# Retention output channel-major in 256-token blocks, PSUM banks given out by the scheduler, and the LRU in three steps

## The chip, the cores and the metric

The kernel runs on the 8 cores of one Trainium2 chip, each core taking one of the 8 sequences of the batch. The metric is the device time of the slowest core, in microseconds (us). Cores 0 to 3 are one die, cores 4 to 7 the other.

Engines are named as in the profile: PE multiplies matrices (PEld loads its weights), DVE is the vector engine, ACT the scalar engine with its function tables (a load of one took 1283 ns in the stage studied below), POOL the GpSimd engine, SP a queue for transfers. PE's results land in PSUM, which the kernel uses as 8 banks of 128 x 512 f32; the program lets PE write a bank again only after another engine has read it out (an *eviction*).

Some executions of this program, whatever the kernel, fall into a slower state, in which a die has a lower granted clock.

## The reference

A layer of a hybrid decoder, per sequence 2048 tokens of 1024 channels. Only the middle part is touched by the change:

```python
x = x + 0.5 * swiglu(rmsnorm(x, ffn1_norm), ffn1_w1, ffn1_w3, ffn1_w2)      # first FFN
h = rmsnorm(x, mix_norm)
u = h @ w_in                                        # q | k | v | g_ret | x_lru | g_lru

# mixer A: retention, 4 heads, dk 128, dv 256
ret = retention_chunkwise(rotary(q, pos), rotary(k, pos), v)   # chunks of 128 tokens and a running state
ret = head_groupnorm(ret, ret_gn)                   # (y - mean) * rsqrt(var + eps) over the 256 of a head
y_ret = (silu(g_ret) * ret) @ w_ret_o

# mixer B: convolution of 4 taps and a gated linear recurrence (called LRU below)
xc = causal_depthwise_conv(x_lru, conv_w, conv_b)
r, i = sigmoid(xc @ w_r + b_r), sigmoid(xc @ w_i + b_i)        # blocks of 128
log_a = -8 * r * softplus(-lam);  a = exp(log_a);  mult = sqrt(1 - a * a)
hl = scan(h_t = a_t * h_(t-1) + mult_t * i_t * xc_t)
y_lru = (hl * gelu(g_lru)) @ w_lru_o

gates = sigmoid(h @ w_branch_gate + b_branch_gate)  # from here on called the tail
x = x + (gates[:D] * y_ret + gates[D:] * y_lru) @ w_out
# ... memory cross-attention, second FFN, final norm
```

## The kernel before

The kernel is written as a list of operations for each engine, with the handles that each reads and writes. A list scheduler in the Python code gives every engine a fixed order: it works with assumed durations and takes, at every step, the operation that can start first. The chip then runs these orders, with semaphores between the engines. PSUM banks are handed out before that, in fixed pools, round robin:

```python
def lru_units():                      # (cut)
    bk = Banks([0, 1])
def ret_steps():
    bkp = Banks([2, 3, 7])            # projections
    bkm = Banks([5, 6])               # scores, outputs, transposes
    SBANK = 4                         # the running state
```

A unit of the LRU is one block of 128 channels and 1024 tokens (16 units), all in one piece:

```python
def unit(u):                          # (cut: only what each engine does)
    # PE: x_lru -> ACT: copy to XL;  DVE: tensor_scalar + 3 scalar_tensor_tensor (conv taps) -> XC
    # POOL: cast to XCB;  PE: g_lru -> ACT: Gelu -> GG (two slots);  PE: gates -> ACT: Tanh -> TR, TI
    dve(lambda e: e.scalar_tensor_tensor(xc.ap, ti.ap, 1.0, xc.ap, ALU.add, ALU.mult), ...)
    act(mu.ap, tr.ap, AF.Exp, ...)
    act(tr.ap, tr.ap, AF.Exp, ...)
    act(mu.ap, mu.ap, AF.Ln, ...)
    act(mu.ap, mu.ap, AF.Exp, ...)    # mu = sqrt(1 - a*a), by Exp and Ln
    pool(lambda e: e.tensor_tensor(mu.ap, xc.ap, mu.ap, ALU.mult), ...)
    prev = XC.v(((u + 1) % 2) * 1024 + 1023, 1)      # last column of the other half of XC
    dve(lambda e: e.tensor_tensor_scan(xc.ap, tr.ap, mu.ap, prev.ap, ALU.mult, ALU.add), ...)
    pool(lambda e: e.tensor_tensor(bt.ap, xc.ap, gg.ap, ALU.mult), ...)
```

Retention is token-major: the output of a chunk is 128 tokens x 2 heads of 256 channels. It is normalised over the free axis and then transposed by PE for the next product:

```python
def fin(p, c, retb, sg, gn_):         # (cut)
    for h in range(2):
        dve(lambda e, h=h: e.bn_stats(...))          # mean and variance of 256 columns
    for h in range(2):
        dve(lambda e, h=h: e.bn_aggr(...))
    dve(lambda e: e.tensor_tensor(s[:, 16:18], mv[:, :, 1], ep, ALU.add), ...)
    pool(lambda e: e.tensor_tensor(s[:, 18:20], s[:, 16:18], ..., ALU.pow), ...)   # (var + eps) ** -0.5
    for h in range(2):
        dve(lambda e, h=h: e.tensor_scalar(rn..., banks[retb]..., mean, rstd, ALU.subtract, ALU.mult), ...)
    pool(lambda e: e.tensor_tensor(at.ap, rn.ap, sg.ap, ALU.mult), ...)

def at_out(p, d, ats):                # 8 transposes on PE, 4 copies with a scale on ACT

def vg(p, c):                         # (cut) value and gate projections of a chunk
    act(sg.ap, banks[outs[1]][:, :], AF.Tanh, [hbk[outs[1]]], sg.hs, 512, tab=S_TANH, scale=0.5)
    dve(lambda e: e.scalar_tensor_tensor(sg.ap, sg.ap, 1.0, banks[outs[1]][:, :], ALU.add, ALU.mult), ...)

for s in range(16):
    unit(s)
    step(s // 8, s % 8)
tail()
```

The softmax here doesn't subtract the row's maximum and nothing guards it: scores larger than these inputs give would overflow.

Of the kernel before, what the change touches and what calls it, by code (L numbers as in the profile page):

```python
# [26 lines left out]
class H:  # L27
    __slots__ = ("name", "lw", "lr")

    def __init__(self, name=""):  # L30
        self.name = name
        self.lw = None
        self.lr = []


class Op:
    __slots__ = ("eng", "fn", "id", "deps", "raw", "cost", "tab", "dma", "succ", "nd", "ready", "fin",
                 "st", "pos", "marked", "idx", "sem", "semval", "prev", "clock", "key")


class Prog:
    def __init__(self):
        self.ops = []

    def add(self, eng, fn, reads=(), writes=(), cost=0.0, tab=None, dma=0, key=None):
        op = Op()
        op.eng, op.fn, op.id, op.cost, op.tab, op.dma = eng, fn, len(self.ops), cost, tab, dma
        op.key = op.id if key is None else key
        deps = {}
        for h in reads:  # L50
            if h.lw is not None:
                deps[h.lw.id] = (h.lw, True)
        for h in writes:
            if h.lw is not None:
                deps[h.lw.id] = (h.lw, True)
            for r in h.lr:
                deps[r.id] = (r, True)
        for h in reads:
            h.lr.append(op)
        for h in writes:  # L60
            h.lw = op
            h.lr = []
        op.deps = [d for d, _ in deps.values()]
        op.raw = {i for i, (_, t) in deps.items() if t}
        self.ops.append(op)
        return op


    def schedule(self):
# [16 lines left out]
        pend = {e: [] for e in ENGS}  # L86
# [5 lines left out]
        cnt = [0]  # L92

        def push(op):
            cnt[0] += 1
            heapq.heappush(pend[op.eng], (op.ready, op.key, cnt[0], op))

        for op in ops:
            if op.nd == 0:
                push(op)  # L100
        left = len(ops)

        def candidate(e):
            p, a = pend[e], avail[e]
            t = tfree[e]
            while p and p[0][0] <= t:
                r, k, c, op = heapq.heappop(p)
                heapq.heappush(a, (k, c, op))
            if e == "act":
                best = None  # L110
                for (k, c, op) in a:
                    pen = TAB_NS + TAB_HOLD if (op.tab is not None and tab[0] is not None and tab[0] not in op.tab) else 0.0
                    cand = (t + pen, k, c, op)
                    if best is None or cand[:3] < best[:3]:
                        best = cand
                for (r, k, c, op) in p:
                    pen = TAB_NS + TAB_HOLD if (op.tab is not None and tab[0] is not None and tab[0] not in op.tab) else 0.0
                    cand = (r + pen, k, c, op)
                    if best is None or cand[:3] < best[:3]:
                        best = cand  # L120
                return best
            if a:
                k, c, op = a[0]
                return (t, k, c, op)
            if p:
                r = p[0][0]
                best = None
                for (rr, k, c, op) in p:
                    if rr <= r + 1e-6 and (best is None or (k, c) < (best[1], best[2])):
                        best = (rr, k, c, op)  # L130
                return best
            return None

        while left:
            sel = None
            for e in ENGS:
                c = candidate(e)
                if c is not None and (sel is None or c[0] < sel[0]):
                    sel = c
                    se = e  # L140
            assert sel is not None, "deadlock"
            st, k, c, op = sel
            a, p = avail[se], pend[se]
            done = False
            for i, x in enumerate(a):
                if x[2] is op:
                    a[i] = a[-1]
                    a.pop()
                    heapq.heapify(a)
                    done = True  # L150
                    break
            if not done:
                for i, x in enumerate(p):
                    if x[3] is op:
                        p[i] = p[-1]
                        p.pop()
                        heapq.heapify(p)
                        break
            st = max(tfree[se], op.ready)
            if se == "act" and op.tab is not None:  # L160
# [5 lines left out]
            tfree[se] = end  # L166
# [4 lines left out]
            op.fin = end  # L171
            op.st = st
            op.pos = len(order[se])
            order[se].append(op)
            left -= 1
            for s in op.succ:
                s.nd -= 1
                lat = 0.0 if (s.eng == op.eng and not op.dma and op.id not in s.raw) else SEM_NS
                if end + lat > s.ready:
                    s.ready = end + lat  # L180
                if s.nd == 0:
                    push(s)
        self.order = order
        self.span = max(op.fin for op in ops)
        return order

    def emit(self, nc):
        order = self.schedule()
# [15 lines left out]
        todo = sorted(self.ops, key=lambda o: (o.fin, o.id))  # L204
# [3 lines left out]
        while n < total:  # L208
            moved = False
            for e in ENGS:  # L210
                while ptr[e] < len(order[e]):
# [9 lines left out]
                    for d in deps:  # L221
# [3 lines left out]
                        else:  # L225
                            if d.eng == e and (e == "pe" or d.id not in op.raw) and not op.dma:
# [81 lines left out]
ARENA_KB = 198  # L308
# [42 lines left out]
T = 2048  # L351
# [14 lines left out]
KB = 1024  # L366

# [7 lines left out]

S_SILU = (18,)
# [4 lines left out]
S_LN = (6,)  # L381

# [20 lines left out]
def build(stage=None):  # L403
    if stage is None:
        stage = STAGE
    nc = bass.Bass("TRN2", target_bir_lowering=False)
    P = Prog()
# [8 lines left out]
    wl_d = dram("w_lru_in", [KC, 128, 2 * KC * 128])  # L416
    wqk_d = dram("w_qk", [2, 128, KC * 512])
    wv_d = dram("w_v", [2, 128, KC * 512])
    wg_d = dram("w_g", [2, 128, KC * 512])
    wgate_d = dram("w_gate", [128, 2 * KC * 128])  # L420
# [12 lines left out]
    v_dr = nc.dram_tensor("v_scr", [128, 4 * 2 * D], BF16).ap()  # L433
    h_park = [H("park%d" % i) for i in range(16)]
# [13 lines left out]
    maskf = fixed("maskf", 128, F32)  # L448
    gam = fixed("gam", 64, F32)
    epst = fixed("epst", 64, F32)  # L450
    cst = fixed("cst", 16, F32)
    wgate = fixed("wgate", 2 * KC * 128, BF16)
    stat_t = nc.alloc_sbuf_tensor("stat", [128, 16 * 4], F32)
    h_stat = [H("stat%d" % i) for i in range(16)]
    rst_t = nc.alloc_sbuf_tensor("rstat", [128, 4 * 24], F32)
    h_rst = [H("rst%d" % i) for i in range(4)]
    io_i = fixed("io_i", 128, I32)
    io_f = fixed("io_f", 128, F32)

    A = Arena(nc, ARENA_KB)  # L460
    banks = [nc.alloc_psum_tensor("bank%d" % i, [128, 512], F32) for i in range(8)]
    hbk = [H("bank%d" % i) for i in range(8)]

    class Banks:
        def __init__(self, ids):
            self.ids = ids
            self.i = 0

        def next(self):
            b = self.ids[self.i % len(self.ids)]  # L470
            self.i += 1
            return b
# [13 lines left out]
    RT = A.buf("RT", 182 * KB, F32, 4 * TB)  # L486
    MT = A.buf("MT", 182 * KB, BF16, KC * MEM)
# [83 lines left out]

    def consts_early():
# [862 lines left out]
```

## Time and profile before

The median was 1898.67 us (1897.75 to 1900.28, three runs). These lines of the profile's page show busy time of each engine over the whole span, and busy tenths in 40 slices of 47.4 us; PEclk is the TensorE clock that was granted, in tenths of full speed.

```profile
PE 1728.3 (91%) x8416; PEld 813.6 (43%) x8584; DVE 906.9 (48%) x1354; ACT 607.0 (32%) x964; POOL 388.3 (20%) x435
...
PE   4999999999987887679688999999999999999997
...
DVE  3476332333486677676785122255553432233355
ACT  3321111112245654565556212135441111111122
...
PEclk9999999999999888889889999999999999999998
```

The average of 91% hides two different kernels. In most slices of the FFNs and the tail PE is busy for 47.0 to 47.2 of 47.4 us at a granted clock of 1.00, so next to nothing is to be gained there. In slices 12 to 22 retention and LRU are mixed (*the stage*): PE falls to 6 to 8 tenths in all but one, its clock to 8 in seven of them, and DVE rises to 5 to 8.

I call *the stage* the time from the end of the first FFN's last matmul to the first matmul that reads the tail's weights. The windows view gives one line for it: start and end, length, then busy us of PE, PEld, DVE, ACT and POOL (with instruction counts), mean PE clock, DMA share and GB/s.

```profile
540.60:1005.80 465.20, 358.60 (x1776) 169.27 (x1808) 333.16 (x480) 261.09 (x406) 200.88 (x149) 0.89 0.11 25
```

PE is busy for 359 of 465 us, and those 359 us include work at half speed (in this core's stage the clock records stand at 0.5 for 106 us, and PE is busy for 59 of them). No other engine is full: the next, DVE, is busy for 333 us. The list of PE's waits in the stage says on whom it waits (us in total, times, longest us):

```profile
PE bank L514 <- DVE SG L1088: 40.9, 9, 8.8
PE bank L1125 <- ACT AT_66 L530: 13.5, 3, 4.7
PE bank L1109 <- DVE RN L1045: 11.7, 7, 4.4
...
```

All three releasers are evictions or belong to the chain behind one. Three answers of the timeline for 904 to 917 us, for PE, ACT and DVE (start, duration, what; in brackets the idle time before it and what ended it):

```profile
906.67 0.38 PE L1155 MATMUL bank<-VS,KT 128*128 128x256 bf16 x2
915.89 1.44 PE L514 MATMUL bank<-hT,RW_76 128*128 128x512 bf16 x3 [8.84 <-DVE SG L1088]
...
908.16 1.14 ACT L530 ACTIVATE MU<-MU,cst 128x1024 f32<-128x1024 f32 x1
...
909.78 1.28 ACT L530 ACT_TABLE_LOAD   x1
911.07 1.09 ACT L530 ACTIVATE GG<-bank 128x512 f32<-128x512 f32 x2
912.04 0.60 ACT L530 ACTIVATE SG<-bank 128x512 f32<-128x512 f32 x1
...
912.81 2.35 DVE L986 TENSOR_TENSOR_SCAN XC<-TR,XC,MU 128x1024 f32<-128x1024 f32 x1 [2.39 <-POOL MU L981]
915.08 0.66 DVE L1088 SCALAR_TENSOR_TENSOR SG<-SG,bank 128x512 f32<-128x512 f32 x1
```

PE's projection wants a bank of its pool of three. The one next in turn holds a gate that ACT's Tanh (SG) and then DVE's multiply must read. ACT is in its Exp and Ln batch for the LRU, has to load the other table (1.28 us), does two Gelus first, and DVE puts a scan of 2.35 us between the Tanh and the multiply. PE stands for 8.84 us.

To count what such standing costs, I measured the distance from the start of each matmul to the start of the next. At full clock 512 columns take 0.216 us (49 of them in 10.74 us in the FFN). A distance longer than that by up to a factor of two is counted as "slow clock" where it is over a quarter too long, and the rest as "idle". This method has a floor of about 14 us of "slow", which it still shows in a run with 2 us at half clock. In medians over the 8 cores, the stage of 464 us was 324 us of matmuls at full speed, 31 us of slow clock and 110 us of idle time.

### The profile page before, as it was taken

The numbers are of one execution on the slowest core, as the hardware profiler recorded it, in microseconds if no ns is written. First come the engines' busy times: TensorE is split into PE (matmuls) and PEld (weight loads), VectorE is DVE, ScalarE is ACT, GpSimd is POOL, SyncE is SP. The second block draws the span as 40 slices with busy tenths as digits, with TensorE's granted clock in tenths as the row PEclk, the third lists the DMA queues.
The fourth block names the chain that finished last, engine by engine and source line by source line (L and its number), as shares of the span: only waits on it lengthen the run. The fifth ranks groups of instructions, "written<-read, shape, count | busy, mean of one in ns | idle before, by whom it ended". The sixth has DMA issues, their size and how long they took to land.

```text
span 1896.1 us, 24126 instructions; the slowest of 8 cores (1883.6 to 1896.1 us)
## 1 busy us (share of the span) xinstructions
PE 1728.3 (91%) x8416; PEld 813.6 (43%) x8584; DVE 906.9 (48%) x1354; ACT 607.0 (32%) x964; POOL 388.3 (20%) x435
## 2 busy tenths in 40 slices
PE   4999999999987887679688999999999999999997
PEld 2444445544443333334233444444444444444443
DVE  3476332333486677676785122255553432233355
ACT  3321111112245654565556212135441111111122
POOL 2101001011114444454446122120010000000000
PEclk9999999999999888889889999999999999999998
DMA  9634136256561110011006321361012221230012
GB/s 222 129 65 103 34 62 95 34 101 137 157 134 23 23 23 13 10 23 23 12 12 132 58 45 31 84 181 57 12 23 45 34 34 34 45 56 12 6 78 100
DMA packets 39286, 118.53 MB, mean 63 GB/s; under 512 B 4480, under 2 KB 4480, under 8 KB 38912
## 3 DMA queue, kind: packets, MB, share of 16 engines
q0 software_dynamic: 23760, 64.50, 21.2%
q1 hardware_dynamic: 15408, 52.48, 8.0%
q8 instruction: 71, 1.16, 0.3%
q14 instruction: 47, 0.39, 0.1%
HBM read 158.38 MB, written 23.07 MB: 96 GB/s over the span
## 4 chain that ended last, share of the span: by engine, by line
PE 82%; DVE 6%; issue 5%; ACT 2%; DMA 2%; POOL 2%; DVEq 0%; SPq 0%; POOLq 0%; ACTq 0%
PE bank L514 79%; PE bank L667 1%; DVE XC L959 1%; DMA ROW<-rows 1%; POOL MU L981 1%; DMA TW<-w_tail 1%; ACT MU L530 1%; POOL rstat L1041 1%; DMA XW<-w_xo 1%; DVE rstat L1035 1%; DVE RN L1045 1%; DVE HB L659 1%; DVE rstat L1040 0%; DVE XC L986 0%; PE bank L1144 0%
## 5 line engine op out<-in xcount | busy, mean ns | idle before, releaser
L514 PE MATMUL bank<-hT,W_45 128*128 128x512 bf16 x2757 | 625.6, 381 | 3.6 <-issue 0.6
L514 PEld LDWEIGHTS bank<-hT,W_45 128*128 128x128 bf16 x2816 | 276.5, 98 | 331.3 <-issue 6.7
L514 PE MATMUL bank<-W_46,HID 128*128 128x512 bf16 x1374 | 319.3, 380 | 5.0 <-DVE HID L738 2.1
L738 DVE TENSOR_TENSOR HID<-bank,STMP 128x512 bf16<-128x512 f32 x176 | 121.7, 691 | 360.8 <-PE bank L514 357.4
L530 ACT ACTIVATE STMP<-bank 128x512 f32<-128x512 f32 x176 | 104.9, 596 | 586.3 <-PE bank L514 580.3
L756 DVE SCALAR_TENSOR_TENSOR X<-bank,X 128x512 f32<-128x512 f32 x256 | 176.4, 691 | 158.9 <-PE bank L514 158.5
L514 PEld LDWEIGHTS bank<-W_46,HID 128*128 128x128 bf16 x1408 | 136.1, 98 | 167.1 <-issue 12.2
L530 ACT ACTIVATE JUNK<-X 128x1024 bf16<-128x1024 f32 x80 | 84.4, 1055 | 163.0 <-DVE X L756 92.6
L1210 DVE SCALAR_TENSOR_TENSOR TT_98<-TT_98,bank 128x512 f32<-128x512 f32 x64 | 44.0, 688 | 164.6 <-PE bank L514 158.9
L651 POOL TENSOR_TENSOR stat<-stat,cst 128x1 f32<-128x1 f32 x82 | 46.1, 564 | 361.7 <-DVE stat L650 361.6
L514 PE MATMUL bank<-hT,TW 128*128 128x512 bf16 x505 | 113.9, 379 | 3.7 <-DMA TW<-w_tail 1.8
L514 PE MATMUL bank<-hT,LW 128*128 128x512 bf16 x501 | 114.8, 382 | 1.3 <-ACT XL L530 0.4
L543 POOL DMA_DIRECT2D W_45<-f_w x44 | 24.2, 552 | 415.7 <-PE bank L514 409.1
L530 ACT ACTIVATE TT_98<-bank,dcol 128x512 f32<-128x512 f32 x64 | 43.7, 687 | 171.1 <-PE bank L514 161.3
L659 DVE SCALAR_TENSOR_TENSOR HB<-X,stat,ROW 128x1024 bf16<-128x1024 f32 x64 | 81.9, 1289 | 19.5 <-POOL stat L651 9.5
L514 PEld LDWEIGHTS bank<-hT,TW 128*128 128x128 bf16 x512 | 49.9, 98 | 63.4 <-issue 4.2
L514 PEld LDWEIGHTS bank<-hT,LW 128*128 128x128 bf16 x512 | 50.1, 99 | 60.1 <-issue 3.1
L1214 POOL TENSOR_TENSOR MG<-TT_98 128x512 bf16<-128x512 f32 x32 | 40.5, 1266 | 158.2 <-DVE TT_98 L1210 147.0
L667 PE MATMUL bank<-identb,HB 128*128 128x128 bf16 x528 | 41.9, 230 | 32.1 <-DVE HB L659 27.7
L514 PE MATMUL bank<-RW_76,hT 128*128 128x512 bf16 x247 | 62.6, 397 | 8.0 <-DVE T_87 L1023 6.3
L514 PE MATMUL bank<-RW_75,hT 128*128 128x512 bf16 x250 | 62.7, 397 | 4.7 <-DVE T_87 L1023 1.9
L959 DVE SCALAR_TENSOR_TENSOR XC<-XL,pc,XC 128x1024 f32<-128x1024 f32 x48 | 62.2, 1296 | 2.0
(188 smaller groups left out, 2007.4 us busy)
## 6 DMA issues: line engine op xcount, KB each, us to landing
W_45<-f_w POOLq DMA_DIRECT2D x44, 512.0 KB, 6.9
W_46<-f_w POOLq DMA_DIRECT2D x44, 256.0 KB, 7.2
X<-x SPq DMA_DIRECT2D x16, 512.0 KB, 10.8
park<-X SPq DMA_DIRECT2D x16, 512.0 KB, 7.0
TW<-w_tail POOLq DMA_DIRECT2D x16, 512.0 KB, 6.8
X<-park SPq DMA_DIRECT2D x16, 512.0 KB, 8.3
out<-OST SPq DMA_DIRECT2D x16, 512.0 KB, 2.6
LW<-w_lru_in POOLq DMA_DIRECT2D x8, 512.0 KB, 5.2
```

The lines of the kernel that those rows point to most:

```text
L514: ins = e.matmul(out_ap, l, r, start=(start and i == 0), stop=(stop and i == n - 1), skip_group_check=skip)
L530: P.add("act", lambda e: e.activation(out, in_, func, **kw), reads=reads, writes=writes, cost=act_cost(n, nap), tab=tab)
L543: P.add("pool", lambda e: e.dma_start(out=out, in_=in_), reads=reads, writes=writes, cost=600, dma=nbytes)
L651: pool(lambda e: e.tensor_tensor(s[:, 2:3], s[:, 1:2], cc(2), ALU.pow), hs + cst.hs, hs, 550)
L659: dve(lambda e: e.scalar_tensor_tensor(hb.ap, src.ap, r, row.ap, ALU.mult, ALU.mult), src.hs + rh + row.hs, hb.hs, D)
L667: ins = e.transpose(bv[:, c * 128:(c + 1) * 128], hb.ap[:, c * 128:(c + 1) * 128], identb.ap)
L738: dve(lambda e: e.tensor_tensor(hd.ap, banks[b3][:, :], s.ap, ALU.mult), [hbk[b3]] + s.hs, hd.hs, TB)
L756: dve(lambda e, b=b, xv=xv: e.scalar_tensor_tensor(xv.ap, banks[b][:, :], 0.5, xv.ap, ALU.mult, ALU.add), [hbk[b]] + xv.hs, xv.hs, 512)
L959: dve(lambda e, s=s: e.scalar_tensor_tensor(xc.ap, XL.v(s, 1024).ap, pcol("conv_w", s * 8 + c), xc.ap, ALU.mult, ALU.add), xl_all.hs + xc. ...
L981: pool(lambda e: e.tensor_tensor(mu.ap, xc.ap, mu.ap, ALU.mult), xc.hs + mu.hs, mu.hs, pool_cost(1024))
L1210: dve(lambda e, t=t, by=by: e.scalar_tensor_tensor(t.ap, t.ap, 1.0, banks[by][:, :], ALU.add, ALU.mult), t.hs + [hbk[by]], t.hs, TB)
L1214: pool(lambda e, d=d, ts_=tuple(ts_): e.tensor_tensor(d.ap, ts_[0].ap, ts_[1].ap, ALU.add), ts_[0].hs + ts_[1].hs, d.hs, pool_cost(TB))
```

## The change

Its intent is to take the token-major round trips out of retention, and to let PE run ahead of the evictions.

- Retention comes out channel-major, in blocks of 256 tokens. The group norm's mean disappears because the value weights are centred over each head once, by DVE in the first FFN. The sum of squares is a matmul with ones, the power is Ln and Exp on ACT, and the result needs no transposes.
- A bank is no longer fixed when the program is written: the scheduler gives one out when PE first touches a tile and takes it back after the last reader.
- An LRU unit is cut into `stA` (convolution and gates), `stG` (Gelu branch) and `stB` (Exp, Ln and scan). `stA` of the next unit is issued before `stB` of this one, and the scan's last column is copied to `hlast`, so that the next convolution needn't wait for it.
- The convolution's first tap moves from DVE to ACT. The slots of the gate (SG) cover 4 x 512 columns and are single-buffered; so is GG.

The core of the diff, cut heavily:

```diff
 class Banks:
-    # fixed list of banks, round robin
+    def next(self):                      # a tile; its bank is chosen by the scheduler
+        v = len(self.prog.tiles)
+        self.prog.tiles.append(self)
+        ...
+        def can_take(op):                # in Prog.schedule, when PE first touches a tile
+            ...
+            b = min(free, key=lambda x: (freeat[x], x))
+            return b, freeat[b] + SEM_NS

-        bk = Banks([0, 1])
+        bk = Banks(P)
-        bkp = Banks([2, 3, 7])
-        bkm = Banks([5, 6])
-        SBANK = 4
+        bkp = Banks(P); bkm = Banks(P, 2); bks = Banks(P); bkstate = Banks(P)

+    def centre_v(h):                     # side job of the first FFN, four times
+        dve(lambda e: e.tensor_reduce(m.ap, w.ap, mybir.AxisListType.X, ALU.add), ...)
+        dve(lambda e: e.tensor_tensor(o.ap, w.ap, mb, ALU.subtract), ...)

-            dve(lambda e: e.tensor_scalar(xc.ap, XL.v(3, 1024).ap, pcol("conv_w", 24 + c), ...
+                act(x2.ap, banks[b][:, :], AF.Identity, ..., bias=pcol("conv_b", c), scale=pcol("conv_w", 24 + c))

+                pool(lambda e: e.tensor_copy(hlast.ap, xc.ap[:, 1023:1024]), xc.hs, hlast.hs, 200)
-                dve(lambda e: e.tensor_tensor_scan(xc.ap, tr.ap, mu.ap, prev.ap, ALU.mult, ALU.add), ...
+                dve(lambda e: e.tensor_tensor_scan(xc.ap, tr.ap, mu.ap, hlast.ap, ALU.mult, ALU.add), ...

-        def fin(...), def at_out(...), def vg(...), def step(...)
+        def gate(p, tb):                 # 4 projections of 512 tokens: Tanh on ACT, multiply on DVE, into SG
+        def block(p, d):                 # 256 tokens, 2 heads
+            # V, scores, KT, SB as before, then for each head:
+            #   PE: VS as weights, scores and q moving -> 2 x 256 columns of one bank
+                act(sq.ap, banks[b][:, :], AF.Square, [hbk[b]], sq.hs, 512, scale=blk_scale(2 * p + h, d))
+                dve(... scalar_tensor_tensor(sg.ap, banks[b][:, ec * 256:(ec + 1) * 256], col, sg.ap, ALU.mult, ALU.mult) ...)
+            #   PE: ones x sq, summed, + eps -> bank bs
+            act(rs.ap, banks[bs][:, :], AF.Ln, [hbk[bs]], rs.hs, 512, tab=S_LN, scale=1.0 / 256.0)
+            act(rs.ap, rs.ap, AF.Exp, rs.hs, rs.hs, 512, tab=S_EXP, scale=-0.5)
+            #   per head, straight into the operand of the next product:
+                pool(lambda e, sa=sa, da=da, rb=rb: e.tensor_tensor(da, sa, rb, ALU.mult), ...)

-        for s in range(16):
-            unit(s)
-            step(s // 8, s % 8)
+        stA(0); stG(0); ret_load(1)
+        qk(0, 0); gate_(0, 0)
+        for u in range(16):
+            if u + 1 < 16: stA(u + 1)
+            stB(u)
+            for f in steps[u]: f()       # a block, and the next qk or gate
+            if u + 1 < 16: stG(u + 1)
```

## The prediction

> **What bounds the kernel now.** The page gives PE 91% busy, and the chain of waits is 79% one line, the shared matmul helper. By window (busy time per stretch) three quarters of the kernel can't gain: in the first FFN, the tail, the cross-attention and the second FFN PE is busy 47.1 of 47.4 us at clock 1.0. The stretch where retention and LRU are mixed (530 to 1042 us, 512 us) is different: PE 400 us, DVE 362, ACT 286, POOL 229, mean clock 0.90, seven slices at 0.82 to 0.90. So 113 us are idle there, and part of the busy time runs slow: in the timeline at 729 us, after an idle of 6.5 us, 512-column matmuls follow each other at 0.43 us, where the FFN's take 0.216 us. [...] Counted at 0.216 us, the stage's matmuls are about 325 us. The list of waits names round trips for PE's idle: above all SG's multiply on DVE (41 us; it frees a fixed bank).
>
> **What the change does, in that stage.**
> - PE: drops 128 output transposes; adds 32 sum-of-squares groups (1536 columns a block) and 768 columns a block for scores and output. Net near +10 us: about 335 to 340 us at full clock.
> - DVE: drops bn_stats 27, bn_aggr 11.5, the epsilon add 16, RN 35, one conv tensor_scalar 27 us; adds 64 multiplies of 256 columns (27 us). From 362 to about 265 to 275 us.
> - POOL: drops 29 us of power and its round trip; about 195 us.
> - ACT: drops 30 us of AT copies and 9 of KT; adds the conv's first tap (32 x 0.69), squares (32 x 0.6), Ln and Exp for the norm (32 x 0.6). Work about 276 us, plus table loads at 1.28 us each (21 in the stage now). Ln/Exp in every block should raise them to 32 to 45, so ACT is about 320 to 330 us: nearly PE's equal, the new second limit.
> - The chains: the LRU is pipelined one unit ahead and eight banks are shared, so matmul groups can run ahead of evictions. That removes most idle time, and with it the half clock.
> - Before the stage: centring the value weights costs some 4 x 5 us on DVE in the first FFN, where DVE is idle over half of the time: nothing, up to 3 us.
>
> **Critical path.** PE needs 340 us, ACT some 325, in fixed orders with dependences; I expect neither to be perfect: the stage takes about 395 to 405 us, 110 us less. The rest stays as it is (start-up idle of 30 us, last 12 us), within 5 us.
>
> **Predicted: 1790 us, 1745 to 1835 with 8 chances in 10.** Faster by over 2%: 0.94; within 2%: 0.05; slower: 0.01.
>
> **What shows the steps right or wrong.** The windows view of the mixing stage: length 370 to 430, PE busy over 85% of it, clock above 0.95. Groups: DVE about 270, ACT 310 to 340 with 32 to 45 table loads. Idle before PE's groups falls from 113 us to 40 to 60. FFN windows unchanged. The waits of PE should name ACT more than DVE.
>
> **What would make it wrong.** Table loads beyond 60 (ACT then bounds the stage at 350 or more); a plan made from assumed durations that the chip doesn't keep, so that fixed orders wait on each other; a single-buffered tile (SG, RS, GG, SB) making a new serial chain; PE gaps long enough to keep the clock low.

512 us less 110 is the stage of about 400 us, and 1898.67 less 110, with the rest unchanged within 5 us, is the 1790 us.

## The result, and the profile after

Four runs of the changed kernel took 1863.3, 1865.45, 1866.74 and 2092.45 us; the last is slow. In the same rounds the kernel before took 1897.37 to 1900.28 us. The ratio is 0.9824, with a 95% interval of 0.9805 to 0.9844: a gain of 33 us, under the 2% that would be called faster. The outputs were correct. Ratios in this document are the mean time of one kernel's fast runs over that of the other's fast runs of the same rounds, so they are not quite the ratio of the medians that are quoted beside them.

The page after, the same lines:

```profile
PE 1742.0 (93%) x8431; PEld 820.8 (44%) x8600; DVE 877.2 (47%) x1277; ACT 637.6 (34%) x978; POOL 387.3 (21%) x415
...
PE   4999999999997988888879999999999999999997
...
DVE  3477444243567567666642212166462332233355
ACT  3421111113346677667762121135452011101132
...
PEclk9999999999998999988989999999999999999999
```

The stage ends some 30 us earlier, PE is at 7 to 8 tenths in most of it and its clock is down to 8 in four slices instead of seven. ACT has risen from 4 to 6 tenths to 6 to 7. The windows view of the stage, after:

```profile
538.50:974.80 436.30, 368.97 (x1815) 175.50 (x1848) 290.42 (x346) 298.73 (x429) 205.31 (x134) 0.92 0.14 30
```

The stage is 29 us shorter. PE's waits in it, the longest in total:

```profile
PE bank L627 <- ACT TR L643: 17.8, 10, 4.4
PE bank L1266 <- ACT TR L643: 6.4, 3, 2.1
PE bank L627 <- ACT RS L643: 5.8, 10, 0.9
...
```

The waits of 40.9, 13.5 and 11.7 us are gone (3.3 us of waiting for the gate's multiply are left). What is left names ACT: an eviction of the LRU's gates (TR) holds a bank. The longest of them in the timeline, from 941 to 955 us, for PE and for ACT:

```profile
944.89 1.03 PE L627 MATMUL bank<-XCB,LW 128*128 128x512 bf16 x4
950.30 3.57 PE L627 MATMUL bank<-hT,RW_77 128*128 128x512 bf16 x8 [4.38 <-ACT TR L643]
...
941.41 1.28 ACT L643 ACT_TABLE_LOAD   x1
942.71 1.24 ACT L643 ACTIVATE MU<-TR,dcol 128x1024 f32<-128x1024 f32 x1
943.86 0.57 ACT L643 ACTIVATE RS<-bank 128x512 f32<-128x512 f32 x1
944.33 1.14 ACT L643 ACTIVATE MU<-MU,cst 128x1024 f32<-128x1024 f32 x1
945.37 1.23 ACT L643 ACTIVATE TR<-TR,dcol 128x1024 f32<-128x1024 f32 x1
946.50 1.14 ACT L643 ACTIVATE MU<-MU,cst 128x1024 f32<-128x1024 f32 x1
947.54 0.62 ACT L643 ACTIVATE RS<-RS 128x512 f32<-128x512 f32 x1
948.17 1.28 ACT L643 ACT_TABLE_LOAD   x1
949.47 0.69 ACT L643 ACTIVATE TR<-bank,dcol 128x512 f32<-128x512 f32 x1
```

From 941.41 to 949.47 ACT evicts nothing but one RS: a table load, six Exp and Ln operations (four of them of over 1.1 us), and a table load back, 8.06 us. PE fills four banks with the LRU's gates by 945.9 and then has no bank: its next projection reads neither TR nor TI, so only the bank makes it wait. After the gap its 8 matmuls take 3.57 us, twice their time at full clock (8 x 0.216 is 1.73 us). The clock record from 948.2 to 955.0 us, which starts 2.3 us into this gap, is at 0.5. All half-clock records of the changed kernel's stage last 3.41, 6.83 or 10.24 us, on all cores. A shorter gap has such a record too. Core 4 has a gap of 2.34 us, from 707.5 to 709.9 us, with shorter ones before it:

```profile
707.14 0.38 PE L627 MATMUL bank<-XCB,LW 128*128 128x512 bf16 x1 [0.49 <-ACT RS L643]
709.86 3.25 PE L627 MATMUL bank<-RW_76,hT 128*128 128x512 bf16 x8 [2.34 <-ACT TR L643]
```

A half-clock record starts at 709.2 us, 1.7 us into this gap, and lasts 3.41 us. The stage has 109 half-clock records on the 8 cores; in the 3.41 us before each of them, PE was idle for 1.74 to 3.30 us, never for all of it.

The account of the stage, in medians over the cores, for all kernels (us; "work" is matmuls at full clock; "at 0.5" is the time of the clock records at half speed; the last columns are busy times and the number of table loads). The names are those of the experiments below. The last gap, just before the tail's first matmul, is left out of "idle" here and of the counts of gaps below: there PE waits for the tail's weights, for up to 4 us in the changed kernel, 3 to 8 us in t_same_order and 6 to 8 us in a_old_chain.

| kernel | stage | work | slow | idle | at 0.5 | DVE | ACT | loads | POOL |
|---|---|---|---|---|---|---|---|---|---|
| before | 464 | 324 | 31 | 110 | 99 | 332 | 261 | 20 | 202 |
| after | 436 | 331 | 40 | 63 | 75 | 289 | 296 | 29 | 206 |
| b_free_banks | 450 | 325 | 47 | 79 | 93 | 340 | 260 | 17 | 210 |
| a_fixed_banks | 472 | 318 | 36 | 117 | 104 | 275 | 297 | 33 | 180 |
| a_old_chain | 461 | 331 | 39 | 83 | 67 | 298 | 304 | 35 | 201 |
| c_new_lru_old_ret | 450 | 322 | 41 | 90 | 84 | 313 | 294 | 28 | 219 |
| a_same_table | 415 | 331 | 22 | 59 | 26 | 292 | 257 | 1 | 206 |
| t_same_order | 412 | 331 | 23 | 53 | 32 | 285 | 262 | 1 | 207 |
| f_pool_copy | 421 | 331 | 33 | 58 | 53 | 264 | 295 | 29 | 109 |
| d_bf16_one_slot | 430 | 331 | 35 | 62 | 63 | 285 | 297 | 29 | 198 |
| d_two_slots | 404 | 329 | 26 | 48 | 44 | 276 | 288 | 25 | 205 |
| e_withheld | 430 | 332 | 33 | 65 | 48 | 287 | 297 | 31 | 213 |
| e_warm | 418 | 377 | 14 | 25 | 2 | 286 | 296 | 31 | 212 |
| h_two_slots_warm | 417 | 376 | 14 | 27 | 3 | 274 | 283 | 23 | 193 |

Outside the stage little moved (medians over cores, before to after): 537.7 to 535.7 us in front of it, 240.3 to 238.8 in the tail, 649.2 to 647.1 behind. The profiled run of the changed kernel was not quite undisturbed: the four cores of die 1 have clock records at 13/16 (0.81), 20 to 45 us on each, where no core has one in the profiled run of the kernel before, and their part behind the tail took 648.4 us where die 0 took 645.7. The slowest core, 4, is one of them (1863.9 us); the slowest of die 0 took 1860.4.

So the change removed 47 us of idle time, but it added 8 us of work and did not remove the slow clock: 31 us became 40. (The clock was at half for less time, 75 us after 99, but PE was busy for 63 us of that where it had been busy for 52.) The rest of this document is about why so much idle time and half clock stayed.

### The profile page after: what moved, and what is told of

The parts are those of the page before. It is cut to its first block, busy times and chain, and to the rows that moved or that the text cites. A ratio compares the mean times of both kernels' runs of the same rounds, so it can differ in the third digit from the quotient of the medians.

```text
span 1863.9 us, 24044 instructions; the slowest of 8 cores (1852.0 to 1863.9 us)
## 1 busy us (share of the span) xinstructions
PE 1742.0 (93%) x8431; PEld 820.8 (44%) x8600; DVE 877.2 (47%) x1277; ACT 637.6 (34%) x978; POOL 387.3 (21%) x415
## 4 chain that ended last, share of the span: by engine, by line
PE 88%; issue 3%; ACT 3%; DVE 3%; DMA 2%; POOL 1%; DVEq 0%; ACTq 0%; POOLq 0%; SPq 0%
PE bank L627 84%; PE bank L838 2%; DMA X<-x 1%; DVE XC L1123 1%; ACT L643 1%; DMA TW<-w_tail 1%; ACT TR L643 1%; DMA XW<-w_xqT 0%; ACT RS L643 0%; DVE HB L830 0%; DVE SG L1306 0%; PE bank L1290 0%; PE bank L1322 0%; PE bank L1293 0%; ACT JUNK L643 0%
## 5 line engine op out<-in xcount | busy, mean ns | idle before, releaser
L627 PE MATMUL bank<-hT,W_45 128*128 128x512 bf16 x2756 | 614.1, 380 | 4.2 <-DVE hT L846 1.0
L627 PE MATMUL bank<-W_46,HID 128*128 128x512 bf16 x1377 | 312.2, 381 | 2.8 <-DVE HID L909 1.0
L627 PE MATMUL bank<-hT,TW 128*128 128x512 bf16 x502 | 122.3, 385 | 0.5
L627 PE MATMUL bank<-hT,LW 128*128 128x512 bf16 x498 | 119.5, 394 | 1.9 <-ACT RS L643 0.9
L1123 DVE SCALAR_TENSOR_TENSOR XC<-XL,pc,XC 128x1024 f32<-128x1024 f32 x48 | 67.9, 1414 | 50.0 <-ACT XL L643 49.3
L627 PEld LDWEIGHTS bank<-hT,LW 128*128 128x128 bf16 x512 | 51.5, 101 | 67.0 <-issue 13.5
L627 PE MATMUL bank<-hT,RW_77 128*128 128x512 bf16 x249 | 61.9, 400 | 9.3 <-ACT TR L643 4.4
L627 PE MATMUL bank<-hT,RW_76 128*128 128x512 bf16 x247 | 58.0, 384 | 2.2 <-ACT GG L643 0.8
```

What stands on the lines that cost most here:

```text
L627: ins = e.matmul(out_ap, l, r, start=(start and i == 0), stop=(stop and i == n - 1), skip_group_check=skip)
L1123: dve(lambda e, s=s: e.scalar_tensor_tensor(xc.ap, XL.v(s, 1024).ap, pcol("conv_w", s * 8 + c), xc.ap, ALU.mult, ALU.add), xl_all.hs + xc. ...
```

## Experiments

The predictions' theories are spelled out in the quoted expectations. In short, the candidates for what was left were: the banks (freed by the scheduler or not), the LRU's old chain, ACT's table loads, POOL and DVE in each other's way, too few buffers, the half clock itself, and mere luck of the order that the scheduler finds.

One thing must be known first. The scheduler's order changes with any change of the program or of its assumed durations. Three kernels below (d_bf16_one_slot, f_pool_copy, t_same_order) keep the order of the changed kernel exactly, position by position on every engine; e_warm and e_withheld have the same order as each other. The others have orders of their own, and the size of that effect was measured too (at the end).

### Free banks alone: b_free_banks

```diff
 # kernel before, with the bank scheduler of the changed kernel
-        bk = Banks([0, 1])
+        bk = Banks(P)
-        bkp = Banks([2, 3, 7])
-        bkm = Banks([5, 6])
-        SBANK = 4
+        bkp = Banks(P); bkm = Banks(P); SBANK = bkstate.next()      # and so in all stages
```

> The kernel before with one part of the change alone: PSUM banks given out by the scheduler (and its order of side work). Retention, LRU and group norm are the old ones. Theory P (what the change is worth lies in the banks, not in the new retention or LRU): about 1865 us, within 10 us of the changed kernel; PE's idle in the mixing stage falls from 115 us to 60 to 75. Theory R (the channel-major retention and the LRU steps take the round trips away, the banks only help): 1885 to 1900 us, at most 13 us better than before.

Measured: 1882.9 and 1883.0 us in two undisturbed runs, against 1893 to 1899 of the kernel before. Two other runs took 1909 and 1911 us; in the profiled one of them, cores 6 and 7 alone ran at 13/16 of the clock for 160 us:

```profile
core 5: 1878.2 us, clock 0.969
...
core 7: 1907.6 us, clock 0.954
```

These two runs count as fast in the ratio of 0.998 (0.989 to 1.007), which is therefore of little use; the six other cores took 1877 to 1879 us. The stage shrank by 14 us: idle time from 110 to 79, but slow clock from 31 to 47. Most of that is a shift of the stage's end, though: the tail's matmuls begin earlier, amid those of the mixing, and the tail takes 251 us instead of 240. From the start to the end of the tail the cores took 1240 us before (median), 1233 here, and 1211 with the whole change. Free banks alone are worth 11 to 15 us, of which some 4 lie behind the tail.

### The new code with fixed banks: a_fixed_banks

```diff
-    def __init__(self, prog, keep=1):
+    def __init__(self, prog, keep=1, ids=tuple(range(8))):
-            b = min(free, key=lambda x: (freeat[x], x))
+            b = min(free & c.ids, key=lambda x: (freeat[x], x))
-        bk = Banks(P)
+        bk = Banks(P, 1, (0, 1))
-        bkp = Banks(P)
-        bkm = Banks(P, 2)
-        bks = Banks(P)
+        bkp = Banks(P, 1, (2, 3))
+        bkm = Banks(P, 2, (5, 6))
+        bks = Banks(P, 1, (7,))           # state 4; the other stages as in the kernel before
```

> The changed kernel with fixed pools of banks again (2 for LRU, 2 for projections, 2 for scores, 1 for the norm sums, 1 for the state, as before elsewhere). Theory P: all of the gain is lost and more: 1900 to 1950 us, as the new retention holds more banks at a time than the old. Theory R: most of the gain stays, 1865 to 1885 us.

Measured: 1930.5 us, ratio 1.018 (1.016 to 1.020), so 32 us *slower* than the kernel before. The stage has 117 us of idle time, and the tail behind it, which overlaps the mixing's last 40 us, takes 268 us instead of 240. The first of PE's waits names the cause:

```profile
PE bank L621 <- ACT GG L637: 52.4, 4, 16.0
```

The sums of squares, for which the projections gave up their third bank, are not among PE's larger waits; the Gelu branch of the LRU is. In three waits of 16 us each, its results fill the LRU's two banks while ACT runs Exp and Ln between two table loads (656.1 to 674.2 us in the first), and PE's next group of that pool stands. So the new code depends on the bank scheduler; it isn't an addition to it.

### The new retention with the LRU's old chain: a_old_chain

```diff
-                pool(lambda e: e.tensor_copy(hlast.ap, xc.ap[:, 1023:1024]), xc.hs, hlast.hs, 200)
-                dve(lambda e: e.tensor_tensor_scan(xc.ap, tr.ap, mu.ap, hlast.ap, ALU.mult, ALU.add), ...
+                prev = XC.v(((u + 1) % 2) * 1024 + 1023, 1)
+                dve(lambda e: e.tensor_tensor_scan(xc.ap, tr.ap, mu.ap, prev.ap, ALU.mult, ALU.add), ...
-            if u + 1 < 16:
-                stA(u + 1)
+            stA(u)
+            stG(u)
             stB(u)
```

> The changed kernel with the LRU's old dependence: the scan reads the last column of the other half's buffer, so the next unit's convolution can't start before the scan; units recorded one after the other. Theory P: small, 1870 to 1885 us (5 to 15 us slower). Theory C (the LRU chain is what bounds the stage): over 30 us slower, 1895 us or more.

Measured: 1889.0 us, ratio 0.996. With free banks and the new retention but the old chain, the kernel is no better than free banks alone (1883). Of the 24 us that it is behind the changed kernel, some 5 may not be the chain's: at the end of its stage, just before the tail's first matmul, PE stands for 6 to 8 us on every core, where it stands for 1 us in the changed kernel (median, at most 4). In the same program in another order (a_old_chain_sem90) the gap is as long, and the profile names the tail's weights for it.

### The new LRU with the old retention: c_new_lru_old_ret

```diff
 # b_free_banks, with the three steps of the changed kernel in place of unit(u)
-            unit(s)
-            step(s // 8, s % 8)
+            stA(s + 1); stB(s); step(s // 8, s % 8); stG(s + 1)
```

> The kernel before with scheduler's banks and the new three-step LRU, but the old token-major retention with bn_stats, power and transposes. If the parts simply add (banks alone 1883 us undisturbed, new LRU chain 24 us): about 1859 us, so the channel-major retention would be worth nothing (-7 us). If the retention rewrite is needed to feed the new LRU's free slots (it takes some 90 us of DVE away): 1875 to 1885 us.

Measured: 1887.7 us, ratio 0.995. The new LRU alone brings nothing over free banks either. The two rewrites only pay together: with both, the time is 22 to 24 us below either of them.

### No table switches: a_same_table and t_same_order

Both give wrong results: ACT's Exp and Ln in the LRU and in the norm become Tanh, which is in the table that the rest of the stage uses (1 load is left of 29). Every operation keeps its size. The first tells the scheduler, which then finds another order; the second doesn't, so that the order of the changed kernel stays and only the loads go.

```diff
-                act(mu.ap, tr.ap, AF.Exp, ..., tab=S_EXP, ...)       # and five more Exp and Ln
+                act(mu.ap, tr.ap, AF.Tanh, ..., tab=S_TANH, ...)     # a_same_table
+                act(mu.ap, tr.ap, AF.Tanh, ..., tab=S_EXP, ...)      # t_same_order: the scheduler isn't told
```

> The changed kernel with every Exp and Ln of the mixing stage replaced by Tanh on the same tiles (wrong result on purpose): same ACT work, no table loads (30 fewer, 38 us of ACT), nothing to batch. Theory T (the Exp/Ln batches keep ACT from emptying banks; 44 us of the 67 us of PE's gaps over 0.6 us overlap such a batch, and the half clock follows them): 40 to 70 us faster, 1795 to 1825 us. Theory P: PSUM stays full of results waiting for single buffers, only 5 to 15 us faster, 1850 to 1860 us.

> The changed kernel, same order on all engines and same banks, every Exp and Ln of the stage replaced by Tanh (wrong result on purpose), so the 29 table loads of the stage fall away and nothing else. Theory T (each load and batch keeps banks full while PE waits): 20 us or more faster, up to the loads' own 37 us, 1829 to 1846 us. Theory P (ACT has slack of its own, a load only hurts where a bank waits for it): 5 to 15 us faster, 1851 to 1861 us.

Measured: a_same_table 1846.3 us (0.974), t_same_order 1840.6 us (0.970 [0.969 to 0.972]). The stage of t_same_order, in the windows view:

```profile
540.40:954.30 413.90, 356.67 (x1848) 171.01 (x1845) 284.77 (x346) 262.05 (x403) 207.41 (x135) 0.96 0.14 30
```

With the order unchanged, taking away 28 of the 29 loads takes away 25 us. The loads as they stand in the changed kernel, by form in the stage (count, then busy us, mean ns, and idle time before them):

```profile
L643 ACT ACT_TABLE_LOAD x29 | 37.2, 1283 | 0.5
```

ACT is busy for only 299 of 436 us, so this isn't ACT being full. PE's gaps of over 0.6 us in the stage fell from 48 of 67 us to 44 of 54 us, and those of over 2 us from 14 to 6; the half clock fell from 75 to 32 us. PE's waits at the projections for TR's evictions fell from 17.8 to 6.5 us. So I read it that a load is dear because evictions queue behind it: ACT at 68% of the stage still makes PE stand when its busy time comes in blocks of 8 us. The run doesn't separate this from the LRU's own chain, which gets its Exp and Ln sooner too. The 25 us are, if anything, a little too few for the loads, as a wait for the tail's weights has grown at the stage's end:

```profile
PE bank L627 <- DMA TW<-w_tail: 6.3, 1, 6.3
```

A load took 1283 ns in the changed kernel's stage, and ACT has no idle time of note around it: in that kernel's timeline above the operation before the load ends at 948.16, the load runs from 948.17 to 949.45, and the next begins at 949.47. The same holds for all 232 loads in the stage on the 8 cores: under 0.02 us idle on either side.

### POOL's two-operand work replaced by copies: f_pool_copy

Its output is wrong, which doesn't matter for the time. POOL's products and sums in the stage become copies of one operand, in the same places and the same order.

```diff
-            pool(lambda e: e.tensor_tensor(mu.ap, xc.ap, mu.ap, ALU.mult), ...)
+            pool(lambda e: e.tensor_copy(mu.ap, xc.ap), ...)           # and BT, the QK sum, and the product with RS
```

> The changed kernel, same order, with POOL's four kinds of multiplies and adds in the stage replaced by copies of one operand (wrong result on purpose; same dependences): POOL does about half of its 206 us. Theory X (DVE and POOL slow each other, as scans went from 2.5 to 3.2 us, the TI multiply from 1.5 to 2.0, POOL's output multiply from 1.27 to 2.3 us, and the plan of the schedule isn't kept for that reason): 15 us or more faster. Theory P: within 8 us of 1866 us.

Measured: 1849.4 us, ratio 0.974, which is 16 us under the changed kernel. DVE's own operations got shorter although nothing about them was changed. From the groups by form, first the kernel before, then the changed kernel, then f_pool_copy:

```profile
L984 DVE TENSOR_TENSOR_SCAN XC<-TR,MU 128x1024 f32<-128x1024 f32 x7 | 17.7, 2528 | 1.2 <-POOL MU L981 1.1
L976 DVE SCALAR_TENSOR_TENSOR XC<-TI,XC 128x1024 f32<-128x1024 f32 x16 | 23.7, 1478 | 6.8 <-ACT TI L530 6.6
```

```profile
L1133 DVE SCALAR_TENSOR_TENSOR XC<-TI,XC 128x1024 f32<-128x1024 f32 x16 | 32.5, 2031 | 10.5 <-ACT TI L643 10.4
L1163 DVE TENSOR_TENSOR_SCAN XC<-TR,hlast,MU 128x1024 f32<-128x1024 f32 x7 | 22.6, 3225 | 2.5 <-POOL MU L1157 2.5
L1336 POOL TENSOR_TENSOR ATP_66<-SG,RS 128x512 bf16<-128x512 f32 x8 | 18.1, 2268 | 4.5 <-ACT RS L643 4.5
L1336 POOL TENSOR_TENSOR ATP_67<-SG,RS 128x512 bf16<-128x512 f32 x8 | 10.1, 1265 | 0.0
```

```profile
L1133 DVE SCALAR_TENSOR_TENSOR XC<-TI,XC 128x1024 f32<-128x1024 f32 x16 | 21.0, 1311 | 18.2 <-ACT TI L643 18.2
L1163 DVE TENSOR_TENSOR_SCAN XC<-TR,hlast,MU 128x1024 f32<-128x1024 f32 x8 | 19.6, 2450 | 6.5 <-POOL MU L1157 6.5
```

The same scan takes 2450 ns in the run with copies and 3225 in that with products; the multiply by TI 1311 against 2031. On POOL, the first product of a pair takes 2268 ns where the second takes 1265. Operations of the two engines take longer where they overlap (called contention here; by which way they hold each other up isn't shown): within the changed kernel's stage alone (all cores), the multiply by TI takes 1224 ns on average where POOL stands and 2427 where POOL is at work for over 80% of it, and POOL's product with RS takes 1266 ns where no DVE instruction that reads two tiles and no bank overlaps it, and 2446 where such instructions do for over half a microsecond. A copy isn't free of it: in f_pool_copy the copies are shorter and meet DVE less often, and in the 8 cases where POOL covered the multiply by TI it took 1975 ns. The change raised this cost: in the kernel before the multiply by TI took 1478 ns and the scan 2528. The 16 us aren't all contention, as the copies also shorten POOL's own part of the chain (206 to 109 us busy).

### Two slots for the gate and the rotary tiles: d_bf16_one_slot and d_two_slots

SG and T12 are single-buffered, and in the kernel's arena (202 KB a partition, of which its tiles leave 3 KB) there is no room for a second f32 slot (8 and 4 KB). In bf16 there is. d_bf16_one_slot changes the type alone, and keeps the order:

```diff
-    T12 = seq("T12", F32, 2 * TB)
+    T12 = seq("T12", BF16, 4 * TB)
-    SG = seq("SG", F32, 4 * TB)
+    SG = seq("SG", BF16, 8 * TB)
```

d_two_slots uses the room for a second slot as well:

```diff
-                t1 = T12.v(0, TB)
-                t2 = T12.v(TB, TB)
+                t1 = T12.v((i % 2) * 2 * TB, TB)
+                t2 = T12.v((i % 2) * 2 * TB + TB, TB)
-                sg = SG.v(i * TB, TB)
+                sg = SG.v((tb % 2) * 4 * TB + i * TB, TB)        # and so where SG is read
```

> Control of the two-slot run: the same two tiles in bf16, but one slot each, order of all engines as in the changed kernel. If the 35 us of the two slots come from the slots (theory P): within 6 us of 1866 us. If they come from the element type (DVE and POOL read and write half the bytes): 1831 to 1845 us.

> The changed kernel with the rotary's two products and the retention gate held in bf16 instead of float32, and in two slots each in the same bytes. Theory P (PE runs ahead, and its results sit in PSUM because the tile that they go to is still in use, so that the banks run out): 15 to 30 us faster, 1836 to 1851 us, PE's idle in the stage from 63 to 40 to 50 us. Theory T (what is left is ACT's Exp/Ln batches, 20 us by the run without tables, and the half clock): within 5 us of 1866 us.

Measured: d_bf16_one_slot 1856.4 us (0.978), d_two_slots **1831.2 us, ratio 0.965 (0.963 to 0.966), correct**. It beats both kernels: 67 us under the one before and 34 under the changed one. Its stage in the windows view, and PE's waits in it:

```profile
539.70:945.00 405.30, 355.69 (x1793) 172.46 (x1825) 276.17 (x337) 288.06 (x419) 203.61 (x135) 0.95 0.14 29
```

```profile
PE bank L627 <- DVE T L1201: 12.4, 8, 4.1
PE bank L627 <- POOL XCB L1126: 5.0, 4, 3.0
PE bank L627 <- ACT GG L643: 3.1, 2, 2.2
...
```

The wait for TR, 17.8 us, is gone from the top of the list (1.7 us are left), although nothing was done to TR: with a second slot the gate's evictions needn't wait for POOL's product of the block before, so ACT comes to the LRU's gates in a better moment. This is my reading of the code, not a measurement. What is measured is that PE's gaps over 0.6 us fell from 48 of 67 us to 37 of 49 us, those over 2 us from 14 to 5, and the half clock from 75 to 44 us. Of the 34 us, 9 come with the type alone, in the same order, and 25 with the slots and the order that they allow, which also has 25 table loads instead of 29. Of the 9 us of the type, a part is the disturbance of die 1 in the changed kernel's run: on die 0 the slowest cores took 1860.4 and 1854.8 us. With the type, POOL's product with RS went from 1898 to 1765 ns and the multiply by TI from 2006 to 1871 (means over all cores), so less contention may be the reason, but no run isolates it. The 34 us are also those of one order: with the assumed latency of 90 ns below, the two slots are worth 16.

### The half clock itself: e_warm, e_withheld and h_two_slots_warm

If the half clock is what costs, useless matmuls in the gaps should win it back. One bank is held for the whole stage, and PE gets such matmuls wherever the schedule's plan has a gap:

```diff
+        fillv = Banks(P).next()
+        # in the schedule, for neighbours x, y in PE's order:
+            n = int(FILL * (y.st - x.fin) / 216.0)     # FILL 0.85; e_withheld has FILL 0.0 (the bank is held, nothing is run)
```

h_two_slots_warm is d_two_slots with FILL 0.85.

> The changed kernel with one PSUM bank withheld in the mixing stage and matmuls of no use written to it where the plan of the schedule foresees PE idle (85% of each such gap). Theory H (the half clock after gaps costs about 40 us of the stage): against the run with the bank withheld alone, 15 to 35 us faster, and the time at clock 0.5 in the stage falls from about 70 us to under 30 us. Rival (the half clock only fills time in which PE would wait anyway, as the stage is paced by ACT and the banks): within 6 us of it, although the clock rises.

> Control of the run above: the same bank withheld, no matmuls added. Theory P: the stage is short of banks, so one bank less costs 8 to 15 us: 1874 to 1881 us. If banks no longer matter at eight: within 4 us of 1866 us.

> Two slots and the matmuls of no use (with their withheld bank) together. If the half clock is a cost of its own: a few us to 12 us faster than two slots alone, 1819 to 1829 us. If the withheld bank or the pacing by other engines takes it back: 1831 to 1845 us.

Measured: e_withheld 1856.7 us (0.978), e_warm 1845.3 (0.972), h_two_slots_warm 1847.5 (0.973). The stage of e_warm and of e_withheld, in the windows view:

```profile
541.10:959.70 418.60, 391.19 (x2062) 188.24 (x2060) 286.61 (x346) 296.32 (x428) 212.31 (x134) 1.00 0.13 28
```

```profile
537.60:970.10 432.50, 359.09 (x1815) 173.01 (x1849) 287.48 (x346) 301.61 (x433) 213.71 (x135) 0.95 0.15 30
```

The clock reads 1.00 and the time at half clock fell from 48 to 2 us, yet the whole kernel gained only 11 us in the same order, where "slow" fell by 19. That lies between the two theories. Some of the full clock was thus spent on useless matmuls or on waiting for the same evictions sooner. On top of two slots it gained nothing (1847 against 1831, in another order). The half clock is thus a consequence of the gaps, since it goes when they are filled. It is not all of the cost: the stage without it is still 418 us. How much it costs by itself isn't shown, as the 45 us of useless matmuls can also hold up useful ones.

### How much the order alone moves: the runs with other assumed latencies

The scheduler assumes 70 ns for a semaphore. Other values leave the program and its dependences the same but give another order: 90 moves 215 of PE's 1326 operations in the changed kernel, 110 moves 244.

```diff
-SEM_NS = 70.0
+SEM_NS = 90.0        # 110.0 in g_sem110
```

> Yardstick: the changed kernel with nothing but the scheduler's assumed semaphore delay changed from 70 to 90 ns, so another order out of the same rules. The run with a bank withheld was 9 us faster where slower was expected; if the order alone moves the time by that much, this run lies 4 to 12 us from 1866 us in either direction, and differences under some 10 us say nothing of a mechanism. If the order is no matter: within 3 us.

> The changed kernel with an assumed semaphore delay of 110 ns, a third order of the same dependences. If the order on record was an unlucky one: 1840 to 1856 us, like the second. If orders scatter: anywhere from 1840 to 1880 us.

> Two slots with the assumed delay of 90 ns. Theory P (slots are worth some 20 us whatever the order): 1822 to 1838 us, at least 10 us under the changed kernel with 90 ns (1851). If the two slots only had a lucky order: 1840 us or more.

> The kernel before with the scheduler's banks alone, assumed delay 90 ns. If banks alone stay short of the changed kernel by the retention and LRU work: 1870 to 1890 us undisturbed. If their 1883 us was an unlucky order: 1850 to 1865 us.

> The kernel before, its own scheduler and fixed banks, assumed delay 90 ns: how far the order alone moves it. Expected within 10 us of 1898 us; if it lies 15 us or more away, the measured ratio of the change is itself partly luck.

> The changed kernel with the LRU's old dependence, assumed delay 90 ns. If the old chain costs what the first order said: 1875 to 1895 us, some 20 us or more over the three orders of the changed kernel (1851 to 1866). If that was an unlucky order: 1855 to 1870 us.

Measured (median of fast runs, us, and ratio to the kernel before in the same rounds):

| program | order at 70 | at 90 | at 110 |
|---|---|---|---|
| before | 1898 | 1898.8 (1.000) | |
| free banks alone | 1883 (undisturbed runs) | 1887.5 (0.995) | |
| new retention, old chain | 1889.0 (0.996) | 1881.5 (0.991) | |
| the change | 1865.5 (0.982) | 1850.7 (0.975) | 1857.6 (0.978) |
| two slots | 1831.2 (0.965) | 1835.0 (0.967) | |

The changed kernel moves by 15 us with nothing but the order, which is half of what the change gained; its verdict of "within 2%" would have been "faster" with the order at 90, and "unclear" with that at 110 (0.976 to 0.980). The kernel before moves by less than 1 us. The two slots are worth 34 us over the change at 70 and 16 at 90. The ranking of the programs holds in both orders, except that free banks alone and the old chain change places. That may be a disturbance: at 90, die 1 of free banks has clock records at 13/16 and took up to 1886 us in the profiled run, die 0 1875 to 1878 us. But a difference of under some 15 us between two kernels of different order proves nothing, and so I take nothing from e_withheld's 9 us under the changed kernel, from h_two_slots_warm's 16 over d_two_slots, or from the 5 to 6 us, in either direction, between free banks alone and either rewrite on top.

## Why the prediction was wrong

The prediction was 1790 us (1745 to 1835), with 0.94 on faster by over 2%. The time was 1866 us. It is off by 76 us and outside the range, and the class was the one given 0.05. Point by point:

- **Where the time could be gained: right.** Outside the mixing stage nothing moved by over about 2 us in the medians of the cores (3.5 us behind the tail on die 0). The centring of the value weights cost nothing: between 94.8 and 189.6 us, PE was busy for 94.33 us before and after, while DVE rose from 64.8 to 69.7 us.
- **The base, 512 us, was too long: 48 us of the error.** The prediction took 530 to 1042 us as the stage. By the bounds used here it was 464 us: 11 us of the window were still matmuls of the first FFN, and in the last 36 the tail's matmuls were already running, for the first 19 or so in the gaps of the mixing. (After the change the tail starts at 974.8 us, when the mixing's matmuls have ended at 970.9; this overlap is gone.) So 141 us of idle time and slow clock were there to be removed, not the 187 of 512 less 325. That is a mistake of reading: a window was bounded by the eye's slices instead of by the first and last instruction of the stage.
- **PE's work: nearly right.** Predicted 335 to 340 us at full clock, measured 331.
- **The step that failed: "That removes most idle time, and with it the half clock."** The sum left 60 us for both, with a clock above 0.95. Measured were 63 us idle and 40 slow, 103 together, at a clock of 0.92. The stage took 436 us instead of about 400, the other 36 us. (48 and 36 make 84; some 6 us gained outside the stage bring it to 78, and the 2 us left are from taking medians over cores here and the slowest core there.) The idle time alone came close to the predicted 40 to 60; it was the half clock that did not go with it. 14 gaps of over 2 us were in the stage before and 14 are in it after, only shorter in sum, and half-clock records stand at most such gaps: counted by idle time between matmuls there are 89 gaps of over 2 us on the 8 cores after the change, of which 54 overlap a half-clock record and 6 more end under 0.3 us before one.
- **ACT's load: a little too high, and wrong in consequence.** Predicted 310 to 340 us with 32 to 45 loads; measured 299 with 29. The prediction treated this as a second limit to be compared with PE's total. Totals weren't the question: 28 loads cost 25 us (same order) at an ACT that is busy for 68% of the stage, and the timeline shows evictions standing behind a batch of Exp and Ln while the banks stay full.
- **DVE: right in direction, a little short.** Predicted 265 to 275 us, measured 290. The difference is the contention with POOL, which stretched the scans (from 2528 to 3225 ns, before to after), the conv taps (1296 to 1414) and the multiply by TI (1478 to 2031); f_pool_copy has 264. POOL was predicted at 195 and measured at 205.
- **What PE's waits name: right.** ACT more than DVE.
- **What was named as a danger: right, but given too little weight.** "A single-buffered tile (SG, RS, GG, SB) making a new serial chain" is what d_two_slots removes for SG and T12, with 34 us in one order and 16 in the other. The stage is then 404 us with a clock of 0.95, which is what was predicted for the change itself; the kernel still takes 1831 us and not 1790, because of the base. "Fixed orders that wait on each other" may be there as well: other orders took up to 15 us less.

What the parts of the change did, as far as it was measured: free banks 11 to 15 us; each rewrite on top of them nothing that stands out of the luck of orders; both together 17 us more than free banks alone in the order at 70 ns, and 37 us more at 90, where some 7 are the disturbance of the run with free banks.

What stays open: what of the 9 us of the type in the same order is the type's, and by which way; how the terms overlap (loads 25, POOL 16, slots 25 can't be added, and no run has them together); and what makes the changed kernel so sensitive to its order when the kernel before isn't.

## What to carry to other kernels

Bound a stage by its first and last instruction before counting what can be gained in it, and separate work at full clock, slow clock and idle time. When an engine that evicts banks is far from full, ask how long its longest block without an eviction is, and how many banks and slots PE can fill meanwhile; a second slot, in bf16 to make room, was worth as much here as the whole change in one order and a third of it in another, and neither half of the rewrite gained anything measurable without the other. When a scheduler makes the order, run each kernel in two or three orders before believing a difference of under one per cent.
